# The start of a two-block forward pass on one core: loads by two queues, products of zeros, a fixed order of the first splits, the bias on GpSimd's queue

## The chip, the cores and the metric

One core of one Trainium2 chip. The metric is device microseconds of one execution, lower is better. The kernel before takes 864.13 us (median of three runs, 862.28 to 865.0).

## The reference, cut to what matters

A first block (neighbourhood attention and a bidirectional gated recurrence, then an MLP) and two further layers follow each other on 256 tokens of 1024 values, in float32. Only its start matters here:

```python
h = concatenate([meta_tokens, x])          # 16 meta tokens and 256 tokens, 1024 values each
a = rms_norm(h, norm_mix)                  # h * (mean(h*h) + eps)^-0.5 * norm_mix
(q_na, k_na, v_na, q_hg, z_f, z_b, i_hg, g_hg, gate_na, gate_hg) = split_cols(a @ w_in)
# neighbourhood attention: s = q k^T * scale + bias(rpb); the keys are a window of tokens and the meta tokens
# the branch hgrn2 ends with  o * gain * silu(g_hg)
```

`k_na` is needed for the meta tokens too (they are keys), `g_hg` is used for the 256 tokens alone.

## The kernel before, in words

**Products.** Float32 operands are split in two parts of type float32r, `hi` (a rounded copy, written by ScalarE) and `lo` (the rest, written by VectorE), and a product is three TensorE products: hi by hi, hi by lo, lo by hi. All weights come as one stream of half units (512 rows by 512 columns, 1 MB), in the order of use: `gh` (columns of g_hg), `kn` (k_na), `qn` (q_na), `vn` and so on, two half units each. `emit_raw` (L215) loads half units into three buffers `raw`, by SyncE's queue; `emit_hl` (L238) splits them by quarters into six buffers `whi`, `wlo` (L252 on ScalarE, L253 on VectorE). `use` (L325) hands a half unit to the products. `gh` is made by `xstat_unit`: x^T chunks are the stationary operand, 24 products of 128x512 for each of two halves of the tokens (L347 to L349). `kn` is made by `wstat_unit`: weights are stationary, x^T chunks with 272 columns (256 tokens and 16 meta tokens) stream, 96 products (L357 to L359).

**The start (L486 to L547).** SyncE's queue loads the first tokens `h[0]` in two halves, the row `grow` (norm_mix), the identity, the weights' first quarter, the second tokens `h[1]`, the second quarter, and so on. TensorE spreads `grow` over the partitions (L496). `norm_in` (L515): ScalarE squares and sums (L438), VectorE adds (L429), GpSimd takes the power -0.5 (L430), VectorE scales both halves of the columns (L525, into `xn`). `split_in` (L528): TensorE transposes four blocks (L406), `split_bank` writes `xh` on ScalarE (L413) and `xl` on VectorE (L414). `meta_in` (L549) does the same for the 16 meta tokens `hm`: L525 into `xnm`, transposes L553, then 16 columns of `xh` and `xl`. `ev_gh` (L562) evicts gh: a tanh on ScalarE (L564), two VectorE operations (L565, L566).

**Bias.** `bias_loads` (L602) loads eight pieces `braw` of the bias table (32 partitions, 8 rows of 133 values for each partition; 133 KB) by SyncE's queue (L608), and GpSimd adds the window mask (L613).

**Order.** Each engine runs its instructions strictly in the order of the program that was built. A scheduler with estimated costs sets that order when the program is built; `tc.issue_after` adds a rule that something comes behind a named instruction. A queue's loads start in the order of their issue.

Of the kernel before, what the change touches and what calls it, by code (L numbers as in the profile page):

```python
# [37 lines left out]
# rows of the vector array (128 values each)  # L38
# [3 lines left out]
def consts():  # L42
# [5 lines left out]
    for i in range(7):  # L48
        # the pairs of tokens that a block of 2^(i+1) tokens has across its middle
        a, b = p[:, None] >> i, p[None, :] >> i  # L50
        c[:, 128 * i:128 * i + 128] = (a ^ b) == 1
# [7 lines left out]
    # [s, t] within a tile: the pairs of a 64-chunk with s <= t, and the next chunk's whole  # L59
    c[:, C_GLA:C_GLA + 128] = p[:, None] <= t[None, :]  # L60
    # [s, t]: 1/16 where s <= t in one 64-chunk
# [7 lines left out]
def kernel(  # L69
# [25 lines left out]
    # Slots that tiles of disjoint lifetimes take in turn: "m0".."m18", and the larger "l0".."l2".  # L95
# [6 lines left out]
    def ta(p=128, n=512, dt=F32):  # L102
        """A short-lived tile of the main stream."""
        return tmp.tile([p, n], dt, name=nm("ta"), tag="ta", bufs=TA)

    def tb(p=128, n=512, dt=F32):
        """A short-lived tile of the work beside it."""
# [5 lines left out]
    def mps():  # L113
        return mp.tile([128, 512], F32, name=nm("mp"), tag="mp")
# [14 lines left out]
    # ------------------------------------------------ constants and vectors  # L129
# [17 lines left out]
    # the activation tables, before the first data  # L147
    S.activation(out=small([128, 1]), in_=zero1, func=AF.Square)

    # ------------------------------------------------ the stream of weights  # L150
    # A half unit is 4 chunks of 128 rows by 512 columns; it is split in two quarters.
# [62 lines left out]
    def emit_raw(n):  # L214
        while st["raw"] < min(n, len(units)):  # L215
# [4 lines left out]
            # the first ones by quarters, which are there sooner  # L220
# [5 lines left out]
    # Quarters that lie in free slots instead of the pool's buffers.  # L226
# [6 lines left out]
    def capped(key):  # L233
        """No splits from the unit key on are emitted."""
# [4 lines left out]
    def emit_hl(i0):  # L239
        """Splits quarters as far as the pool's buffers go, from quarter i0 on."""  # L240
# [17 lines left out]
    # Steps of an eviction that need TensorE again wait for the products of the next half unit.  # L258
# [20 lines left out]
    def flushed(n):  # L279
        """The deferred steps come here on TensorE, before the products of the body."""  # L280
# [8 lines left out]
    # Work beside the stream of products; that of lbg has the lowest priority.  # L289
# [23 lines left out]
    def group():  # L313
        """A group of the stream's products: behind the products beside it of LAG groups ago."""
# [13 lines left out]
    def use(key, budget=None):  # L328
        """The four row chunks (hi, lo) of the next half unit, with the work ahead emitted."""
# [21 lines left out]
    def wstat(ps, xs, ws, b, first, last):  # L351
        """ps[cols, tokens] += weight chunks (stationary, block b of 128 columns) by x^T chunks."""
# [49 lines left out]
    def transposes(src, n=4):  # L402
        """[128 tokens, n*128] -> one bank [128, n*128] of transposed blocks."""
# [6 lines left out]
    def split_bank(ps, hi, lo, scale=None):  # L410
        """hi and lo (f32r views) of a bank, or of a float32 tile, of the same shape."""
# [1225 lines left out]
```

## Time and profile before

| | |
|---|---|
| median of three runs (862.28 to 865.0) | 864.13 us |
| profiled execution, span from its first to its last instruction | 864.1 us |
| profiled execution, its own time: no figure apart from the span, nothing is listed around it | 864.1 us |
| TensorE products, busy | 841.6 us, 97% of the span |
| VectorE, busy | 583.3 us, 68% |
| ScalarE, busy | 463.2 us, 54% |
| GpSimd, busy | 57.4 us, 7% |
| mean granted TensorE clock | 0.995 |

How to read it: the start of the span is 0 in all views. A row of the view in order of time gives the start, the duration, the engine (PE TensorE, PEld its weight loads, DVE VectorE, ACT ScalarE, POOL GpSimd, SPq SyncE's queue), the line, the operation, output<-inputs, how many, and in brackets the idle time before it and what ended it. TensorE's products overlap: the distance from one start to the next is what one of them takes. Shares are means over stages, so a stage is read in its own window.

### The profile page before, as it was taken

Reading aid. Unit: us, or ns where it says so; the run is one execution under the profiler, and the core shown is the slowest. Engines: PE = TensorE matmul, PEld = TensorE weight load, DVE = VectorE, ACT = ScalarE, POOL = GpSimd, SP = SyncE. Lnnn points to the kernel's source line nnn. Section 1 sums busy time; section 2 is a strip of 40 time slices with the busy share of each in tenths; the row PEclk is TensorE's granted clock in tenths of the full one; section 3 lists DMA queues with packets and bytes.
Section 4 is the critical chain, followed back from the end, with each engine's and each line's share of the span. In section 5 each row is a group of like instructions: output and inputs, shape, how many; then the busy total and the mean of one; then the engine's idle time right before and its main releaser. Section 6 shows DMA issues by size and latency. Waiting matters only on the chain.

```text
span 864.1 us, 12274 instructions
## 1 busy us (share of the span) xinstructions
PE 841.6 (97%) x4757; PEld 726.7 (84%) x4757; DVE 583.3 (68%) x838; ACT 463.2 (54%) x743; POOL 57.4 (7%) x134
## 2 busy tenths in 40 slices
PE   6999999999999999999999999989999999999996
PEld 4899998887888888888888988868789999888885
DVE  6746637983858996787666777788756556656643
ACT  6546545655547545556666545444567544555532
POOL 1700001001000000000011000000000000010001
PEclk9999999999999999999999999999999999999999
DMA  8964415441457998777627556988445444535521
GB/s 272 282 216 129 138 49 196 149 144 50 157 209 266 382 372 293 256 283 241 214 87 238 188 179 217 313 270 266 148 171 174 168 148 146 183 110 178 188 98 49
DMA packets 88974, 168.84 MB, mean 195 GB/s; under 512 B 4770, under 2 KB 9250, under 8 KB 88916
## 3 DMA queue, kind: packets, MB, share of 16 engines
q1 hardware_dynamic: 88244, 167.51, 57.4%
q8 instruction: 37, 0.61, 0.3%
q10 hardware_dynamic: 288, 0.52, 0.2%
q14 instruction: 21, 0.17, 0.1%
q0 software_dynamic: 384, 0.03, 0.0%
HBM read 167.00 MB, written 1.05 MB: 194 GB/s over the span
## 4 chain that ended last, share of the span: by engine, by line
PE 86%; DMA 7%; DVE 3%; ACT 2%; issue 1%; SPq 0%; POOL 0%; POOLq 0%; DVEq 0%; ACTq 0%
PE acc L347 15%; PE acc L348 15%; PE acc L349 15%; PE acc L357 6%; PE acc L358 6%; PE acc L359 6%; DMA adw<-in_ada_w_dram 4%; PE mp L347 3%; PE mp L348 3%; PE mp L349 3%; PE mp L406 3%; DMA raw<-in_w_in_dram 2%; PE mp L829 1%; DVE wlo L253 1%; DMA lvf<-in_cst_dram 1%
## 5 line engine op out<-in xcount | busy, mean ns | idle before, releaser
L253 DVE TENSOR_TENSOR wlo<-raw,whi 128x1024 fp32r<-128x1024 f32 x244 | 295.3, 1226 | 142.7 <-ACT whi L252 140.8
L252 ACT ACTIVATE whi<-raw 128x1024 fp32r<-128x1024 f32 x244 | 253.6, 1056 | 188.6 <-PE acc L349 94.6
L461 DVE SCALAR_TENSOR_TENSOR tb<-adw,csil,tb 128x512 f32<-128x512 f32 x96 | 70.8, 747 | 11.4 <-DMA adw<-in_ada_w_dram 10.3
L359 PE MATMUL acc<-xh,wlo 128*128 128x272 f32 (+1 forms) x224 | 65.2, 293 | 1.2 <-DVE wlo L253 1.2
L357 PE MATMUL acc<-xh,whi 128*128 128x272 f32 (+1 forms) x224 | 65.0, 292 | 0.5 <-DVE kT L637 0.3
L358 PE MATMUL acc<-xl,whi 128*128 128x272 f32 (+1 forms) x224 | 64.9, 291 | 0.0
L359 PE MATMUL acc<-oh,wlo 128*128 128x256 f32 x192 | 55.0, 287 | 0.0
L358 PE MATMUL acc<-ol,whi 128*128 128x256 f32 x192 | 54.6, 284 | 0.0
L357 PE MATMUL acc<-oh,whi 128*128 128x256 f32 x192 | 54.4, 283 | 0.0
L348 PE MATMUL acc<-wlo,yT 128*128 128x512 f32 (+1 forms) x128 | 49.1, 384 | 3.4 <-DVE wlo L253 3.4
L348 PE MATMUL acc<-wlo,hh 128*128 128x512 f32 x128 | 50.6, 395 | 0.0
L349 PE MATMUL acc<-whi,hl 128*128 128x512 f32 x128 | 50.5, 395 | 0.0
L347 PE MATMUL acc<-whi,hh 128*128 128x512 f32 x128 | 50.3, 393 | 0.0
L347 PE MATMUL acc<-whi,yT 128*128 128x512 f32 (+1 forms) x128 | 49.1, 385 | 0.0
L349 PE MATMUL acc<-whi,yT 128*128 128x512 f32 (+1 forms) x128 | 48.8, 383 | 0.0
L359 PEld LDWEIGHTS acc<-xh,wlo 128*128 128x128 f32 x224 | 42.8, 192 | 2.1 <-DVE wlo L253 1.6
L348 PE MATMUL acc<-wlo,oh 128*128 128x512 f32 x112 | 44.5, 397 | 0.0
L347 PE MATMUL acc<-whi,oh 128*128 128x512 f32 x112 | 44.2, 394 | 0.0
L349 PE MATMUL acc<-whi,ol 128*128 128x512 f32 x112 | 44.1, 394 | 0.0
L357 PEld LDWEIGHTS acc<-xh,whi 128*128 128x128 f32 x224 | 42.8, 192 | 1.6 <-issue 0.6
L347 PE MATMUL mp<-whi,uh 128*128 128x512 f32 x112 | 43.9, 394 | 0.0
L348 PE MATMUL acc<-wlo,eh 128*128 128x512 f32 x112 | 43.9, 392 | 0.0
(406 smaller groups left out, 1950.6 us busy)
## 6 DMA issues: line engine op xcount, KB each, us to landing
raw<-in_odd_in_w_dram SPq DMA_DIRECT2D x28, 1024.0 KB, 5.0
adw<-in_ada_w_dram SPq DMA_DIRECT2D x48, 512.0 KB, 6.4
raw<-in_w_in_dram SPq DMA_DIRECT2D x21, 1024.0 KB, 5.2
raw<-in_even_in_w_dram SPq DMA_DIRECT2D x20, 1024.0 KB, 5.0
raw<-in_w_up_dram SPq DMA_DIRECT2D x16, 1024.0 KB, 6.6
raw<-in_w_down_dram SPq DMA_DIRECT2D x16, 1024.0 KB, 7.5
raw<-in_even_out_w_dram SPq DMA_DIRECT2D x8, 1024.0 KB, 5.8
raw<-in_odd_out_w_dram SPq DMA_DIRECT2D x8, 1024.0 KB, 5.0
```

Source lines behind the costliest of these rows:

```text
L252: S.activation(out=hi.rearrange("p k n -> p (k n)"), in_=r, func=AF.Copy)
L253: V.tensor_tensor(out=lo.rearrange("p k n -> p (k n)"), in0=r, in1=f(hi.rearrange("p k n -> p (k n)")), op=ALU.subtract)
L347: T.matmul(ps, lhsT=xh, rhs=wh, start=first and k == 0, stop=False)
L348: T.matmul(ps, lhsT=xh, rhs=wl, start=False, stop=False)
L349: last_mm[:] = [T.matmul(ps, lhsT=xl, rhs=wh, start=False, stop=last and k == n - 1)]
L357: T.matmul(ps, lhsT=wh[:, c], rhs=xh, start=first and k == 0, stop=False)
L358: T.matmul(ps, lhsT=wh[:, c], rhs=xl, start=False, stop=False)
L359: T.matmul(ps, lhsT=wl[:, c], rhs=xh, start=False, stop=last and k == n - 1)
L406: last_t[:] = [T.transpose(out=ps[:, 128 * b:128 * b + 128], in_=src[:, 128 * b:128 * b + 128], identity=ident)]
L461: V.scalar_tensor_tensor(out=a, in0=w[:, k], scalar=csil[:, kk:kk + 1], in1=a, op0=ALU.mult, op1=ALU.add)
L829: T.matmul(pss[i][:, 128 * hd:128 * hd + 128], lhsT=Kc[:, hd, 128 * i:128 * i + 128], rhs=bass.AP(tensor=q.tensor, offset=q.offset, ap=ap[ ...
```

## The change

- `h[0]` (two halves) and `h[1]` are loaded by ScalarE's queue; SyncE's queue begins with `grow`, the first quarter of weights, the identity and the second quarter. The activation table is loaded behind the three issues.
- TensorE runs ten products of zeros (128x256, bf16) before the products with `grow` and twelve behind them, each behind the one before.
- `norm_in` is cut in two, `sums_in` and `scale_in`. `in_turn` runs a step so that its instructions on all engines are issued behind the last ScalarE and VectorE instruction of the step before it. The first steps (sums, scalings, the first four quarters, the transposes with their splits) are written in one order with it, and `meta_in` is the last step of that order.
- The splits of later quarters, and those of a small gate weight `glw`, come behind the last step (`behind`, `started`).
- The eight loads of the bias go to GpSimd's queue, behind the cast of `lvl` (which waits for the load of `lvf`).

```diff
-    S.activation(out=small([128, 1]), in_=zero1, func=AF.Square)
...
-    nc.sync.dma_start(out=h[0][:, 0:512], in_=x[0:128, 0:512])
+    for c in (slice(0, 512), slice(512, 1024)):
+        nc.scalar.dma_start(out=h[0][:, c], in_=x[0:128, c])
+    nc.scalar.dma_start(out=h[1], in_=x[128:256])
     nc.sync.dma_start(out=grow, in_=vecs[R_MIX:R_MIX + 8].rearrange("(a r) c -> a (r c)", a=1))
-    nc.sync.dma_start(out=h[0][:, 512:1024], in_=x[0:128, 512:1024])
-    nc.sync.dma_start(out=ident, in_=cst[:, C_ID:C_ID + 128])
...
     nc.sync.dma_start(out=w0v[:, 0:2], in_=units[0][1][:, 0:2])
-    nc.sync.dma_start(out=h[1], in_=x[128:256])
+    nc.sync.dma_start(out=ident, in_=cst[:, C_ID:C_ID + 128])
     nc.sync.dma_start(out=w0v[:, 2:4], in_=units[0][1][:, 2:4])
...
+    def warm_up(n):
+        ps = mps()
+        for _ in range(n):
+            with after(first):
+                first[:] = [T.matmul(ps[:, 0:256], lhsT=warm[:, 0:128], rhs=warm, start=True, stop=True)]
+    warm_up(10)
...
+    warm_up(12)
...
-    norm_in(0, h[0], 2)
-    first_split(1)
-    split_in(0, 0)
-    first_split(2)
-    norm_in(1, h[1], 1)
-    split_in(1, 0)
-    first_split(3)
-    split_in(0, 1)
-    first_split(4)
-    split_in(1, 1)
+    turn = {}
+    def in_turn(step, *args):
+        traced = nc.cur_bb.bb.instructions
+        n = len(traced)
+        with ExitStack() as es:
+            for ins in turn.values():
+                es.enter_context(tc.issue_after(ins))
+            r = step(*args)
+        for k in nc.cur_bb.bb.instructions[n:]:
+            if k.engine in (S.engine, V.engine):
+                turn[k.engine] = k
+        return r
+    r0 = in_turn(sums_in, 0, h[0], 2)
+    in_turn(scale_in, 0, h[0], r0, 0)
+    in_turn(first_split, 1)
+    r1 = in_turn(sums_in, 1, h[1], 1)
+    in_turn(split_in, 0, 0)
+    in_turn(scale_in, 1, h[1], r1, 0)
+    in_turn(first_split, 2)
+    in_turn(split_in, 1, 0)
+    for t, r in ((0, r0), (1, r1)):
+        in_turn(scale_in, t, h[t], r, 1)
+        in_turn(first_split, 3 + t)
+        behind[:] = in_turn(split_in, t, 1)
+    started = list(behind)
...
     xstat_unit([("gh", 0), ("gh", 1)], xT, ev_gh)
-    meta_in()
+    in_turn(meta_in)
...
-                nc.sync.dma_start(out=raw[32 * r:32 * r + 32], in_=src)
+                with after([lvl_made]):
+                    nc.gpsimd.dma_start(out=raw[32 * r:32 * r + 32], in_=src)
...
-    split_bank(glw, glr[:, :, 0:16], glr[:, :, 16:32])
+    with after(started):
+        split_bank(glw, glr[:, :, 0:16], glr[:, :, 16:32])
```

What it does to the order of the instructions. **VectorE, where the meta tokens are scaled**, in the program before (`xnm` is the scaled meta tokens, `whi`/`wlo` quarters of weights, `xl` the lower parts of x^T, `raw_114` the first half unit of kn):

```order
L253 TENSOR_TENSOR wlo_169<-raw_108,whi_168 128x1024
L253 TENSOR_TENSOR wlo_180<-raw_108,whi_179 128x1024
L429 TENSOR_REDUCE sm_271<-sm_267 16x1
L414 TENSOR_TENSOR xl_9_118<-mp_161,xh_8_117 128x4x128
L525 SCALAR_TENSOR_TENSOR xnm_123<-hm_111,sm_272,mp_100 16x512
L525 SCALAR_TENSOR_TENSOR xnm_123<-hm_111,sm_272,mp_101 16x512
L253 TENSOR_TENSOR wlo_196<-raw_114,whi_195 128x1024
L414 TENSOR_TENSOR xl_11_120<-mp_172,xh_10_119 128x4x128
```

and in the changed one (line 250 is the line 253 of before, 426 is 429, 411 is 414, 540 is 525, 600 and 601 are 565 and 566; `raw_138` and `raw_253` are the two half units of kn, `raw_338` the first of qn, `acc_219` and `acc_220` the sums of gh):

```order
L250 TENSOR_TENSOR wlo_222<-raw_138,whi_221 128x1024
L250 TENSOR_TENSOR wlo_226<-raw_138,whi_225 128x1024
L250 TENSOR_TENSOR wlo_256<-raw_253,whi_255 128x1024
L250 TENSOR_TENSOR wlo_260<-raw_253,whi_259 128x1024
L426 TENSOR_REDUCE sm_297<-sm_293 16x1
L411 TENSOR_TENSOR glr<-glw,glr 128x8x16
L600 SCALAR_TENSOR_TENSOR gg_216<-gg_216,acc_219 128x512
L600 SCALAR_TENSOR_TENSOR gg_216<-gg_216,acc_220 128x512
L601 TENSOR_TENSOR gg_216<-gg_216,hgn_b 128x512
L250 TENSOR_TENSOR wlo_341<-raw_338,whi_340 128x1024
L601 TENSOR_TENSOR gg_216<-gg_216,hgn_b 128x512
L540 SCALAR_TENSOR_TENSOR xnm_149<-hm_135,sm_298,mp_118 16x512
```

The scaling of the meta tokens stood among the first splits, ahead of kn's; it now stands behind all four splits of kn, the eviction of gh and one split of qn.

**TensorE, where gh ends and kn begins**, in the changed program (lines 344 to 346 are 347 to 349 of before, 354 to 356 are 357 to 359, 588 is 553; `vrow` is a table of vectors):

```order
L346 MATMUL acc_220<-whi_205,xl_14_146 128x512
L588 MATMUL mp_303<-ident,xnm_149 128x16 x4
L610 MATMUL mp_320<-ident,vrow 128x128
L588 MATMUL mp_303<-ident,xnm_149 128x16 x4
L354 MATMUL acc_348<-xh_11_143,whi_221 128x272
L354 MATMUL acc_349<-xh_11_143,whi_221 128x272
L354 MATMUL acc_350<-xh_11_143,whi_221 128x272
L354 MATMUL acc_351<-xh_11_143,whi_221 128x272
L355 MATMUL acc_348<-xl_12_144,whi_221 128x272
```

Before, the transposes of the meta tokens stood within gh, with 22 of its 48 products still to come; now nothing of gh is left behind them, and kn's products, which read the meta tokens' columns, follow at once.

**GpSimd**, in the changed program (427 is the power, 430 before; 608 is the cast of `lvl`):

```order
L427 TENSOR_TENSOR sm_170<-sm_169,mhalf 128x1
L608 CAST lvl<-lvf_317 128x896
L644 DMA braw_484<-in_na_rpb_dram 32x8x133
L644 DMA braw_509<-in_na_rpb_dram 32x8x133 x2
L644 DMA braw_484<-in_na_rpb_dram 32x8x133 x2
L644 DMA braw_509<-in_na_rpb_dram 32x8x133
L644 DMA braw_484<-in_na_rpb_dram 32x8x133
L644 DMA braw_509<-in_na_rpb_dram 32x8x133
L427 TENSOR_TENSOR sm_298<-sm_297,mhalf 16x1
```

The eight issues now stand ahead of the meta tokens' power, which before had only the two powers of the tokens in front of it. From the first products of qn on, the order on every engine is that of before (one product of qn stands some places later).

## Rows read from the trace of the kernel before

**Rows 1.** The page's head and its first part: span; busy time, share of the span and number of instructions of each engine.

```profile
span 864.1 us, 12274 instructions
PE 841.6 (97%) x4757; PEld 726.7 (84%) x4757; DVE 583.3 (68%) x838; ACT 463.2 (54%) x743; POOL 57.4 (7%) x134
```

**Rows 2.** Who TensorE waited for, whole span, three of the list, longest first: us in total, times, longest.

```profile
PE acc L348 <- DVE wlo L253: 3.4, 1, 3.4
PE acc L347 <- ACT xh L413: 2.5, 1, 2.5
PE acc L359 <- DVE wlo L253: 1.2, 2, 0.8
```

**Rows 3.** Stretches of 1 us: length, busy time (instructions) of PE, PEld, DVE, ACT, POOL, then the granted clock, the DMA engines' busy share, GB/s.

```profile
6.00:7.00 1.00, 1.00 (x2) 0.00 (x0) 0.22 (x2) 0.01 (x1) 0.55 (x1) 1.00 0.65 215
9.00:10.00 1.00, 0.00 (x0) 0.00 (x0) 0.59 (x1) 0.68 (x2) 0.00 (x0) 1.00 1.04 401
```

**Rows 4.** In order of time, the chain to the first product of gh.

```profile
0.72 1.28 ACT L148 ACT_TABLE_LOAD   x1 [0.72 <-PEq L1626]
3.51 0.63 ACT L438 ACTIVATE junk<-h 128x512 bf16<-128x512 f32 x1 [1.29 <-DMA h<-in_x_dram]
7.74 1.12 PE L406 MATMUL mp<-ident,xn 128*128 128x128 f32 x4 [0.66 <-DVE xn L525]
9.69 1.06 ACT L438 ACTIVATE junk<-h 128x1024 bf16<-128x1024 f32 x1 [0.32 <-DMA h<-in_x_dram]
11.38 0.80 PE L347 MATMUL acc<-whi,xh 128*128 128x512 f32 x1 [2.52 <-ACT xh L413]
```

**Rows 5.** In order of time, TensorE: products with the row of the norm, then products of gh (two places).

```profile
3.33 3.75 PE L496 MATMUL mp<-grow,one_row 1*128 1x512 f32 x4 [3.33 <-DMA grow<-in_vecs_dram]
12.40 0.63 PE L349 MATMUL acc<-whi,xl 128*128 128x512 f32 x1
12.83 0.63 PE L347 MATMUL acc<-whi,xh 128*128 128x512 f32 x1
16.29 0.39 PE L347 MATMUL acc<-whi,xh 128*128 128x512 f32 x1
16.52 0.39 PE L348 MATMUL acc<-wlo,xh 128*128 128x512 f32 x1
```

**Rows 6.** Groups by line and shape, from 0 to 26 us: busy us, mean ns of one, idle us before.

```profile
L253 DVE TENSOR_TENSOR wlo<-raw,whi 128x1024 fp32r<-128x1024 f32 x6 | 7.1, 1214 | 1.1 <-ACT whi L252 1.1
L252 ACT ACTIVATE whi<-raw 128x1024 fp32r<-128x1024 f32 x6 | 6.3, 1051 | 2.9 <-DMA raw<-in_w_in_dram 2.9
L414 DVE TENSOR_TENSOR xl<-mp,xh 128x512 fp32r<-128x512 f32 x4 | 2.7, 676 | 0.3 <-ACT xh L413 0.3
L413 ACT ACTIVATE xh<-mp 128x512 fp32r<-128x512 f32 x4 | 2.3, 573 | 0.0
L525 DVE SCALAR_TENSOR_TENSOR xnm<-hm,sm,mp 16x512 f32<-16x512 f32 x2 | 1.4, 732 | 0.1
L566 DVE TENSOR_TENSOR gg<-gg,hgn_b 128x512 f32<-128x512 f32 x1 | 0.7, 693 | 0.0
```

**Rows 7.** In order of time, the meta tokens and the first product of kn.

```profile
17.48 1.39 DVE L525 SCALAR_TENSOR_TENSOR xnm<-hm,sm,mp 16x512 f32<-16x512 f32 x2
17.48 0.65 PE L406 MATMUL mp<-ident,xn 128*128 128x128 f32 x4
20.86 0.67 PE L553 MATMUL mp<-ident,xnm 16*128 16x16 f32 x8
24.40 0.41 PE L357 MATMUL acc<-xh,whi 128*128 128x272 f32 x2
```

**Rows 8.** In order of time, the loads and splits of kn's second half unit, kn's products from the 50th (35.10) to the 96th and last (40.89), and the first product of qn.

```profile
13.95 5.16 SPq L608 DMA_DIRECT2D braw<-in_na_rpb_dram  x7
20.88 0.39 SPq L222 DMA_DIRECT2D raw<-in_w_in_dram  x1
35.10 0.28 PE L359 MATMUL acc<-xh,wlo 128*128 128x272 f32 x1
40.89 0.29 PE L359 MATMUL acc<-xh,wlo 128*128 128x272 f32 x1
41.45 0.35 PE L357 MATMUL acc<-xh,whi 128*128 128x256 f32 x1 [0.27 <-DVE kT L637]
```

**Rows 9.** From issue to landing, us (smallest, median, largest): the half units issued from 22 to 30 us; the one issued at 38.4 us.

```profile
DMA to landing us min/median/max: 11.1/11.2/11.2
DMA to landing us min/median/max: 5.2/5.2/5.2
```

**Rows 10.** In order of time, TensorE behind its longest wait.

```profile
575.15 0.80 PE L348 MATMUL acc<-wlo,yT 128*128 128x512 f32 x1 [3.36 <-DVE wlo L253]
576.17 0.63 PE L348 MATMUL acc<-wlo,yT 128*128 128x512 f32 x1
576.59 0.63 PE L349 MATMUL acc<-whi,yT 128*128 128x512 f32 x1
578.30 0.53 PE L347 MATMUL acc<-whi,yT 128*128 128x512 f32 x1
```

**Rows 11.** A split on VectorE in order of time, while GpSimd adds the bias; and the loads that GpSimd issues (ns smallest/median/largest, first and last start).

```profile
35.46 1.52 DVE L253 TENSOR_TENSOR wlo<-raw,whi 128x1024 fp32r<-128x1024 f32 x1
L453 POOL DMA_DIRECT2D tb<-in_ada_b_dram x12: 487/487/736, 139.9 to 473.2; - x12
```

More of the change, by code (lines that the diff above doesn't have):

```diff
@@ L487 @@
     grow = mt(10, [1, D], name="grow")
-    nc.sync.dma_start(out=h[0][:, 0:512], in_=x[0:128, 0:512])
+    for c in (slice(0, 512), slice(512, 1024)):
+        nc.scalar.dma_start(out=h[0][:, c], in_=x[0:128, c])
+    nc.scalar.dma_start(out=h[1], in_=x[128:256])
     nc.sync.dma_start(out=grow, in_=vecs[R_MIX:R_MIX + 8].rearrange("(a r) c -> a (r c)", a=1))
-    nc.sync.dma_start(out=h[0][:, 512:1024], in_=x[0:128, 512:1024])
-    nc.sync.dma_start(out=ident, in_=cst[:, C_ID:C_ID + 128])
     one_row = cp.tile([1, 128], F32, name="one_row")
-    G.memset(one_row, 1.0)
-    g_ps = [mps() for _ in range(2)]
-    for k in range(2):
-        T.matmul(g_ps[k], lhsT=one_row, rhs=grow[:, 512 * k:512 * k + 512], start=True, stop=True)
+    V.memset(one_row, 1.0)
     w0 = rawp.tile([128, 2048], F32, name="raw0", tag="raw")
@@ L504 @@
     emit_raw(2)
+    warm = mt(12, [128, 256], BF16, name="warm")
+    V.memset(warm, 0.0)
+    first = []
+    def warm_up(n):
[4 more added lines that the diff above has]
+    warm_up(10)
+    g_ps = [mps() for _ in range(2)]
+    for k in range(2):
+        with after(first):
+            first[:] = [T.matmul(g_ps[k], lhsT=one_row, rhs=grow[:, 512 * k:512 * k + 512], start=True, stop=True)]
+    warm_up(12)
     hm = mt(4, [16, D], name="hm")
@@ L508 @@
     emit_raw(NRAW)
+    S.activation(out=small([128, 1]), in_=zero1, func=AF.Square)
     xT = [(mt(0, [128, 4, 272], F32R, "xh0"), mt(1, [128, 4, 272], F32R, "xl0")),
@@ L513, with sums_in @@
     xn = [mt(5, [128, D], name="xn0"), mt(6, [128, D], name="xn1"), mt(7, [16, D], name="xnm")]
-    def norm_in(t, src, parts):
-        p = src.shape[0]
-        q = small([p, 3])
+    def sums_in(t, src, parts):
+        q = small([src.shape[0], 3])
         G.memset(q, EPS)
@@ L521, in norm_in, with scale_in @@
             sq_mean(src[:, n * i:n * i + n], q[:, i:i + 1], D)
-        r = rpow(q[:, 0:parts + 1])
-        for i in range(2):
-            c = slice(512 * i, 512 * i + 512)
-            V.scalar_tensor_tensor(out=xn[t][:, c], in0=src[:, c], scalar=r, in1=g_ps[i][0:p],
-                                   op0=ALU.mult, op1=ALU.mult)
+        return rpow(q[:, 0:parts + 1])
+    def scale_in(t, src, r, i):
+        c = slice(512 * i, 512 * i + 512)
+        V.scalar_tensor_tensor(out=xn[t][:, c], in0=src[:, c], scalar=r, in1=g_ps[i][0:src.shape[0]],
+                               op0=ALU.mult, op1=ALU.mult)
     def split_in(t, g):
@@ L530, in split_in @@
         c = slice(128 * t, 128 * t + 128)
-        split_bank(ps, xT[g][0][:, :, c], xT[g][1][:, :, c])
+        return split_bank(ps, xT[g][0][:, :, c], xT[g][1][:, :, c])
     def first_split(n):
@@ L536, in first_split @@
         cap[0] = 1 << 30
-    norm_in(0, h[0], 2)
-    first_split(1)
-    split_in(0, 0)
-    first_split(2)
-    norm_in(1, h[1], 1)
-    split_in(1, 0)
-    first_split(3)
-    split_in(0, 1)
-    first_split(4)
-    split_in(1, 1)
+    turn = {}
[23 more added lines that the diff above has]
+    started = list(behind)
     def meta_in():
-        norm_in(2, hm, 1)
+        r = sums_in(2, hm, 1)
+        for i in range(2):
+            scale_in(2, hm, r, i)
         ps = mps()
@@ L572 @@
     nc.sync.dma_start(out=lvf, in_=cst[:, 0:896])
-    G.tensor_copy(out=lvl, in_=lvf)
+    lvl_made = G.tensor_copy(out=lvl, in_=lvf)
     pv = mps()
```

## The prediction

> **What bounds the kernel now.** I read the page's head first: TensorE is busy 97% of the span [rows 1], so only what delays its products counts. The list of its waits comes next: of the waits that it names, 2.5 us stand before the first product of gh and 1.2 us in kn [rows 2]; the largest, 3.4 us, ends at 575.15 [rows 10], in a place that the change does not touch. So I then read the start in order of time, and there three things are to be seen. First, the chain to the first product: the second tokens arrive at 9.7, ScalarE squares them, and only then makes the first tokens' `xh`, whose transposes were done at 8.9; gh begins at 11.38 [rows 4]. Second, TensorE's level: gh's products start 0.43 us apart at 12.4 and 0.23 us apart at 16.3, the 1.2 and the 2.4 GHz levels (the granted clock is listed as 1.00 in both places, so the distances decide) [rows 3, 5]. Third, the bias: its loads stand in SyncE's queue ahead of kn's second half unit, which is issued at 20.88 and not at 13.95 [rows 8]. Behind the first product of qn, at 41.45, the order of everything is unchanged, and TensorE has hardly a gap to give. My forecast is therefore the shift of that one moment.
>
> **The sum.** Its base is the profiled execution, span 864.1 us, which stands at the median of the three runs.
>
> *The loads.* Of the three issues on ScalarE's queue, some 0.4 us each, then the table load, 1.28 us, the end comes at about 3.4, where the first tokens arrived before (3.51) [rows 4]: no cost. What counts is when `h[1]` lands. It cannot be worked out from one row. From 6 to 7 us the engines of the loads were busy 65% at 215 GB/s, with loads waiting, and from 9 to 10 full at 401 [rows 3]. If two queues fill them from the first packet (about 1.6), the 1 MB of tokens and as much of the weights beside them take 5.2 us: 6.9. If they change nothing, it stays 9.7. I take the middle, 8.2. The Trainium skill ("DMA: Bandwidth & Descriptors", section "Issuing engines are not separate DMA queues") says that loads from several engines run on the same 16 DMA engines and that only the sequencer's issue time is saved; by it `h[1]` would stay at 9.7 and the sum below be 1.5 us higher, while the 65% above leave room for more.
>
> *The first product* follows the landing by 11.38 - 9.69 = 1.7 us [rows 4]: 9.9.
>
> *The products of zeros* run from about 1.4 on, beside loads that nothing else waits for, and with the 3.75 us of the norm's row [rows 5] they keep TensorE at work until 8 or 9.5. That does bring a gain: I count gh at 0.23 us. Before, seven products at 0.43 [rows 5] and eight transposes cost some 1.9 us more; if the level falls again before gh, this comes back, 0 to 1.9.
>
> *gh in the fixed order.* `xh` takes 0.57, `xl` 0.68, a split 1.05 on ScalarE and 1.21 on VectorE, a scaling 0.73 [rows 6], four transposes 0.65 to their last result [rows 7]. Seven products and a wait of 0.3 for `xl`: 11.8. VectorE does `xl`, the second tokens' scaling and a split from 9.9 on: 12.5. Seventeen products, 3.9: 16.5. Transposes of the first tokens' second half, 0.65, and `xh`, 0.57: 17.7. Seven products and a wait of 0.3: 19.6. Transposes of the last piece and their `xh`: 20.9. Seventeen more products, which wait until 20.4 for a split, end gh at 24.3, against 27.0 before. So far the change wins almost 3 us.
>
> *The meta tokens.* kn's products read their columns. Before, VectorE scaled them at 17.48 and TensorE transposed them at 20.86, in the midst of gh, so that kn could begin at 24.40 [rows 7]. Now VectorE has the following in its queue behind `xl` of the last piece: four splits of kn, each behind its ScalarE half (first 20.9 + 1.05 = 21.9), 4.85 us: 26.8; two small ones, 0.5; three operations of gh's eviction, 0.69 each: 29.3; the first split of qn, 1.21: 30.5; the last operation of the eviction: 31.2; and only then the two scalings, 1.46: 32.7 [rows 6]. Another split (1.21) and a copy (0.27) stand before the first `xl` of the meta columns, 0.2: 34.4. Transposes and `xh` lie within that. TensorE has its last product of gh at 24.3 and nothing of kn that may run: it stands for about 9 us, but for four products that need `xh` alone. The rest of kn, 92 products at (40.89 - 35.10) / 46 = 0.126 us [rows 8], takes 11.6: qn begins at 46.0 and not at 41.45. **+4.6 us.**
>
> *The bias* no longer delays kn's weights; the second half unit is issued at about 13 and is there by 20. But VectorE is late by then, so this gives nothing beyond the 1.2 us of waits [rows 2], which the walk above no longer holds. GpSimd's queue has the eight issues ahead of the meta tokens' power: the cast of `lvl` ends at about 18.2, and with the 0.49 to 0.74 us of the nearest issues [rows 11] the eight are done by 24.1; the power is needed at 31.2. Cover 7 us, cost nothing; with issues above 1.6 us it is gone (below).
>
> *The clock behind the pause.* After a wait of 3.36 us TensorE's products ran 0.42 us apart until 578.3, 3.1 us [rows 10]; at the start it took from 11.38 to a point ahead of 16.29 [rows 4, 5], about 4 us. At 0.43 for 0.23, such a stretch loses 1.4 to 1.9 us; a pause of 9 us is longer than either needs. I take **+1.7**, between 0 (the level holds) and 1.9.
>
> *VectorE beside GpSimd.* The bias's additions now fall on 28 us and later, where VectorE is the bound; a split beside them took 1.52 for 1.21 [rows 6, 11]. On the 5 to 6 us of VectorE behind 28 that is 0 to 1.4; I take **+0.4**, as not every operation there showed it.
>
> *qn's first half unit* is issued when a raw buffer comes free, at about 20.4, and lands 5.2 to 11.2 us later [rows 9]: 25.6 to 31.6. ScalarE needs it at 27.9. 0 to 3.7; the bias's loads share the engines for part of it: **+0.4**.
>
> Sum: 4.6 + 1.7 + 0.4 + 0.4 = 7.1. **864.1 + 7.1 = 871.2 us**, 0.8% slower. About 0.3%, 2.6 us, is what a measurement of this kernel can tell from no change. Lowest: `h[1]` at 6.9 (-1.3), level held (-1.7), the last two at zero (-0.8): 867.4. Highest: `h[1]` at 9.7 (+1.5), gh at the low level (+1.9), the late half unit (+3.3), the rest 1.2: 879, which wants all at once; three of the four give 877.
>
> **The rivals.**
>
> *GpSimd's issues become the bound.* Each of the eight loads has 256 pieces where the load in the row has few; if an issue takes 2.0 us, the eight end at 34.2, the power at 34.8, and the scaling starts 3.6 us later: 874.8. For it: the row's 0.49 to 0.74 is for loads of 2 KB. Against: it needs more than twice the row's largest. Chance 0.12.
>
> *The other side: the meta tokens are not late.* If VectorE reached their scaling before gh's end (by 23.5), TensorE would go on with a pause of about 1.3 us for the transposes and the two splits of their columns, and qn would begin at 24.3 + 1.3 + 12.1 = 37.7: -3.7, 860.4 us. For it: gh ends almost 3 us sooner, and kn's weights wait for nothing. Against: VectorE's queue has 9.3 us of work between the last `xl` and the scaling, and it does not pass anything; the point from which it decides is that these 9.3 us would have to begin before 14.2. Chance 0.06.
>
> *Nothing to measure.* All at its lowest, 867.4, and the wait of 3.36 us at 571.8, which hangs on a load's landing, does not come back: 864.0. For it: such a wait depends on when loads meet. Against: everything there is shifted together. Chance 0.10, a third of it still above 0.3%.
>
> **How the numbers follow.** The forecast has 0.72. Slower by over 0.3%: 0.72 + 0.12 + 0.03 = 0.87; within 0.3%: 0.07; faster: 0.06. The range 867.5 to 877 takes in the forecast's bounds and the first rival; outside lie faster and same, 0.13, and a little above 877.
>
> **What would show it.** In the profile after: the first product of gh at 8.7 to 11.4, gh's products 0.23 us apart from the first on, gh's end at 23 to 26. Then TensorE's longest wait of the start, 7 to 10 us, ended by VectorE's scaling of `xnm`; VectorE without a gap from about 22 to 33; the first products of kn 0.23 us apart (the low level for kn, twice 0.126 less a little), then 0.126; qn's first product at 46 to 51. Whether the eight issues on GpSimd end before its power for the meta tokens is wanted, and qn's half unit before 28, settles two terms each by a row. I am wrong if kn begins within 3 us of gh's end, or if qn's first product comes later and the end does not.

## The result, and the profile after

The changed kernel takes 873.06 us (median of four runs, 872.36 to 876.98), the kernel before 863.29 us (four runs, 862.28 to 865.0): ratio 1.0114, interval 1.0085 to 1.0143, so 7.3 to 12.3 us slower. The forecast was 871.2 in a range of 867.5 to 877. The profiled execution has a span of 870.4 us and a time of 872.36; wherever a run lists both, the time stands about 2 us above the span. For the profile of before no time was listed, and I had set its span, 864.1, equal to its time. By that difference it was an execution of about 866 us (an estimate), some 2.5 us above the median.

The page's first part, to be held against [rows 1]:

```profile
span 870.4 us, 12333 instructions
PE 846.6 (97%) x4779; PEld 729.6 (84%) x4779; DVE 583.5 (67%) x840; ACT 462.8 (53%) x743; POOL 58.4 (7%) x141
```

TensorE is busy 97% as before and 5 us longer: the shares tell nothing. Whom TensorE waited for (us in total, times, longest), against [rows 2]:

```profile
PE mp L588 <- DVE xnm L540: 8.2, 1, 8.2
PE acc L345 <- DVE wlo L250: 1.5, 1, 1.5
```

One wait of 8.2 us heads the list, for the scaled meta tokens, where before the entries shown were 3.4, 2.5 and 1.2 us; the second entry is the wait at 582 that is spoken of below. TensorE in order of time, against [rows 4, 5, 7, 8]:

```profile
7.27 2.74 PE L509 MATMUL mp<-warm 128*128 128x256 bf16 x12
9.81 1.00 PE L403 MATMUL mp<-ident,xn 128*128 128x128 f32 x4
11.49 0.50 PE L344 MATMUL acc<-whi,xh 128*128 128x512 f32 x1 [0.69 <-ACT xh L410]
12.56 0.40 PE L344 MATMUL acc<-whi,xh 128*128 128x512 f32 x1
12.79 0.39 PE L345 MATMUL acc<-wlo,xh 128*128 128x512 f32 x1
...
25.67 0.40 PE L346 MATMUL acc<-whi,xl 128*128 128x512 f32 x1
34.29 0.58 PE L588 MATMUL mp<-ident,xnm 16*128 16x16 f32 x4 [8.22 <-DVE xnm L540]
36.12 1.27 PE L354 MATMUL acc<-xh,whi 128*128 128x272 f32 x4 [0.31 <-ACT xh L410]
...
50.63 0.28 PE L354 MATMUL acc<-xh,whi 128*128 128x256 f32 x1
```

gh ends at 26.1, kn begins at 36.12, qn at 50.63 and not at 41.45: 9.2 us later. VectorE over the same stretch shows why:

```profile
22.60 0.69 DVE L411 TENSOR_TENSOR xl<-mp,xh 128x512 fp32r<-128x512 f32 x1 [0.80 <-ACT xh L410]
23.55 4.63 DVE L250 TENSOR_TENSOR wlo<-raw,whi 128x1024 fp32r<-128x1024 f32 x4 [0.26 <-ACT whi L249]
...
28.36 1.27 DVE L600 SCALAR_TENSOR_TENSOR gg<-gg,acc 128x512 f32<-128x512 f32 x2
29.56 0.67 DVE L601 TENSOR_TENSOR gg<-gg,hgn_b 128x512 f32<-128x512 f32 x1
31.36 1.23 DVE L250 TENSOR_TENSOR wlo<-raw,whi 128x1024 fp32r<-128x1024 f32 x1 [1.14 <-ACT whi L249]
32.51 0.99 DVE L601 TENSOR_TENSOR gg<-gg,hgn_b 128x512 f32<-128x512 f32 x1
33.42 1.39 DVE L540 SCALAR_TENSOR_TENSOR xnm<-hm,sm,mp 16x512 f32<-16x512 f32 x2
```

From the end of the last `xl` to the start of the scaling `xnm` pass 10.1 us. They hold other work, in the order that the program was built with, and two gaps, of 0.26 and 1.14 us. Stretches of the change (length, busy time and count of PE, PEld, DVE, ACT, POOL, granted clock, DMA share, GB/s): the pause, the first part of kn, the rest of kn.

```profile
26.00:34.00 8.00, 0.07 (x1) 0.00 (x0) 6.87 (x10) 4.55 (x8) 3.58 (x5) 0.82 1.04 294
36.00:41.00 5.00, 4.88 (x21) 4.88 (x22) 2.06 (x10) 0.62 (x4) 5.00 (x15) 0.50 0.71 222
41.50:50.50 9.00, 9.00 (x73) 9.00 (x72) 3.44 (x9) 3.51 (x7) 1.66 (x5) 1.00 0.22 55
```

The pause costs twice: TensorE stands, and then it runs kn's first products at half the clock (1.2 GHz). GpSimd, and then the two places where ScalarE waited for a load, the first tokens' second half and qn's half unit:

```profile
18.51 0.93 POOL L608 CAST lvl<-lvf 128x896 uint8<-128x896 f32 x1 [7.41 <-DMA lvf<-in_cst_dram]
19.39 4.86 POOL L644 DMA_DIRECT2D braw<-in_na_rpb_dram  x8
28.32 0.57 POOL L427 TENSOR_TENSOR sm<-sm,mhalf 16x1 f32<-16x1 f32 x1 [4.07 <-DVE sm L426]
30.98 12.18 POOL L649 TENSOR_TENSOR bias<-braw,cs 128x160 f32<-128x160 f32 x24 [2.10 <-DMA braw<-in_na_rpb_dram]
```

```profile
6.88 0.63 ACT L435 ACTIVATE junk<-h 128x512 bf16<-128x512 f32 x1 [2.36 <-DMA h<-in_x_dram]
...
30.28 2.00 ACT L249 ACTIVATE whi<-raw 128x1024 fp32r<-128x1024 f32 x2 [1.73 <-DMA raw<-in_w_in_dram]
```

The eight issues take 0.61 us each and end at 24.25, 4 us before the meta tokens' power could run: it waits for VectorE, not for the issues. VectorE's gap of 1.14 us comes from qn's half unit: ScalarE waited for its landing and began to split it at 30.28.

Behind qn's first product not all was given on. The profiles are 9.1 us apart where TensorE's wait at 572 begins (581 in the change), and 6.3 at the end: in the change the wait at 582 is 1.46 us and no half clock follows, where before it was 3.36 us with a slow stretch [rows 10]. The first experiment asks whether that belongs to the change.

### The profile page after: what moved, and what is told of

The parts are those of the page before. It is cut to its first block, busy times and chain, and to the rows that moved or that the text cites. A ratio compares the mean times of both kernels' runs of the same rounds, so it can differ in the third digit from the quotient of the medians.

```text
span 870.4 us, 12333 instructions
## 1 busy us (share of the span) xinstructions
PE 846.6 (97%) x4779; PEld 729.6 (84%) x4779; DVE 583.5 (67%) x840; ACT 462.8 (53%) x743; POOL 58.4 (7%) x141
## 4 chain that ended last, share of the span: by engine, by line
PE 84%; DVE 5%; DMA 5%; ACT 3%; issue 2%; POOL 0%; POOLq 0%; ACTq 0%; DVEq 0%
PE acc L344 14%; PE acc L346 13%; PE acc L345 13%; PE acc L354 7%; PE acc L355 7%; PE acc L356 7%; DMA adw<-in_ada_w_dram 3%; PE mp L344 3%; PE mp L346 3%; PE mp L345 3%; PE mp L403 3%; DVE tb L458 1%; DVE wlo L250 1%; PE mp L865 1%; DMA raw<-in_w_in_dram 1%
## 5 line engine op out<-in xcount | busy, mean ns | idle before, releaser
L344 PE MATMUL acc<-whi,yT 128*128 128x512 f32 (+1 forms) x128 | 48.5, 380 | 0.0
L355 PEld LDWEIGHTS acc<-xl,whi 128*128 128x128 f32 x224 | 43.9, 196 | 0.2 <-issue 0.2
```

The source lines that it names most:

```text
L344: T.matmul(ps, lhsT=xh, rhs=wh, start=first and k == 0, stop=False)
L355: T.matmul(ps, lhsT=wh[:, c], rhs=xl, start=False, stop=False)
```

## The experiments

Each ran against the kernel before on the same chip in five rounds. Single executions of one kernel spread by 5 us and more, so an interval is about 0.2% to either side (0.3% in runs 9 to 11, with six executions each).

**1. The kernel before, again.** No edit.

> The kernel before, unchanged. Open: the profiled executions differ by 6.3 us (870.4 against 864.1), the medians by 9.8. Theory A: TensorE's wait of 3.36 us at 571.8 and the 3.4 us at half the clock behind it stand in the profiled execution of before and not in most others (the profile of the change has 1.5 us and no half clock there); then most spans here lie at 860 to 862.5 with a mean clock of 0.997, and those that have it at 863 or more with 0.995. Theory B: every execution has it, clock 0.995 and spans of 863 to 865 throughout, and the 3.5 us have another cause. Ratio 1.000 by both.

863.84 us, ratio 1.0011 (0.9992 to 1.0029). The profile has a span of 860.6, a wait of 1.60 us at 572.87 and no half clock there. Over its 12 executions the mean clock lies anywhere between 0.993 and 0.998, so neither theory is met in its numbers: the slow stretches come and go from one execution to the next. The 3 us given back behind 572 in the profile of the change therefore need not be an effect of the change, and 9.2 us at qn stands beside 9.8 us of the medians.

**2. The meta tokens out of the order.** The change with one word taken back.

```diff
-    in_turn(meta_in)
+    meta_in()
```

> The change with one word taken back: the meta tokens are not a step of the fixed order. Theory M (the meta tokens' scaling stands too far back in VectorE's queue, that is the whole loss): it is done before 20, kn begins within 1.5 us of gh's end, no stretch at half the clock at 31, qn's first product at 39 to 41.5 and not at 50.6: 860 to 864 us, ratio to before 0.996 to 1.001. Rival Q (the queues, the zeros or the loads on GpSimd cost it): the pause goes, and still qn begins at 45 or later, over 867 us, ratio above 1.004.

865.65 us, ratio 1.0033 (1.0015 to 1.0050), 7.4 us less than the change's median (7.0 by the two ratios). TensorE now waits for `xnm` nowhere. Its transposes come at 23.85, kn follows gh at once (28.84), qn's first product is at 43.84, between the two forecasts. But within kn TensorE still waits twice for the meta columns:

```profile
30.85 0.39 PE L355 MATMUL acc<-xl,whi 128*128 128x272 f32 x1 [1.60 <-DVE xl L411]
38.19 0.39 PE L355 MATMUL acc<-xl,whi 128*128 128x272 f32 x1 [0.78 <-DVE xl L411]
```

Their small `xl`, at 30.59 and 37.93, stand behind splits of kn and of qn in VectorE's queue. So the position of the meta tokens is most of the loss. The 2.4 us at qn that are left are not all the rest of the change: the place of these two `xl` is part of them.

**3. The meta tokens early in the order.**

```diff
     in_turn(split_in, 1, 0)
+    r2 = in_turn(sums_in, 2, hm, 1)
...
         in_turn(first_split, 3 + t)
-        behind[:] = in_turn(split_in, t, 1)
+        if t == 0:
+            for i in range(2):
+                in_turn(scale_in, 2, hm, r2, i)
+        in_turn(split_in, t, 1)
...
+    behind[:] = in_turn(meta_in)
...
-    in_turn(meta_in)
```

> The change with the meta tokens as early steps of the fixed order: their sums behind the second quarter, their scaling behind the third, their transposes and splits last, and kn's splits behind them. Theory M: VectorE does the scaling in its idle 17.2 to 19.3 at no cost, gh ends at 26 to 27, kn follows within 0.7 us at the full clock, qn's first product at 38.5 to 40: 2 to 3 us less than before, 859.5 to 862 us, ratio 0.995 to 0.999. Rival Q: above 867. If VectorE's two scalings (1.46 us) cannot lie beside TensorE's work, gh ends 1.4 us later and the ratio is 0.999 to 1.000.

862.14 us, ratio 0.9984 (0.9966 to 1.0002). qn's first product at 41.05. The fixed order is no loss by itself. But gh's last product starts at 28.42, where its end was forecast at 26 to 27. The level came up only at 15.29, for 10.62 in the change, so gh's first seven products are 0.43 us apart. The square of the meta tokens stands ahead of the third quarter's split on ScalarE, which puts that split on VectorE at 18.24 and the scaling `xnm` at 20.13, ahead of an `xl` for which TensorE then waits:

```profile
22.17 0.50 PE L346 MATMUL acc<-whi,xl 128*128 128x512 f32 x1 [0.72 <-DVE xl L411]
```

The longest wait of this profile for `wlo`, 2.35 us, lies at 572, far behind the start.

**4. Two queues alone.** The kernel before with the tokens on ScalarE's queue; SyncE's queue then begins with `grow` and the first quarter, and the table load comes behind ScalarE's three issues, as in the change.

```diff
-    nc.sync.dma_start(out=h[0][:, 0:512], in_=x[0:128, 0:512])
+    for c in (slice(0, 512), slice(512, 1024)):
+        nc.scalar.dma_start(out=h[0][:, c], in_=x[0:128, c])
+    nc.scalar.dma_start(out=h[1], in_=x[128:256])
...
```

> The kernel before with the tokens on ScalarE's queue and nothing else of the change. Theory L (two queues move the first MB sooner, but the weights then share the engines with the first tokens): the first tokens' second half at 6.9 and not at 5.3, the second tokens before 8 and not at 9.7; without the fixed order ScalarE has a split of weights ahead of the square of that second half, so the first product comes at 11.5 to 12.5 against 11.38: ratio 0.999 to 1.002. Rival R (what the Trainium skill states in 'DMA: Bandwidth & Descriptors': engines that issue are not separate queues of transfer): the second tokens stay at 9.7, ratio 1.000 to 1.001. Rival G (more bytes early are a gain): first product at 10, ratio 0.998.

863.61 us, ratio 0.9997 (0.9977 to 1.0018); first product at 11.80. The first 5.5 us of loads, first before, then here:

```profile
1.50:7.00 5.50, 3.67 (x4) 1.16 (x4) 0.22 (x2) 2.15 (x6) 1.41 (x17) 1.00 0.68 213
```

```profile
1.50:7.00 5.50, 3.75 (x4) 1.16 (x4) 0.00 (x0) 3.06 (x5) 0.86 (x16) 1.00 0.92 301
```

ScalarE's squares of the first tokens' second half and of the second tokens:

```profile
7.11 0.61 ACT L437 ACTIVATE junk<-h 128x512 bf16<-128x512 f32 x1
...
8.22 1.06 ACT L437 ACTIVATE junk<-h 128x1024 bf16<-128x1024 f32 x1 [0.41 <-DMA h<-in_x_dram]
```

Two queues fill the 16 engines 92% instead of 68%, and the second tokens are there by 8.2, not 9.7. The Trainium skill ("DMA: Bandwidth & Descriptors", section "Issuing engines are not separate DMA queues") says that issuing from several engines saves only the sequencer's issue time. The trace does not agree: from 5 to 7 us, with loads waiting in both kernels, the DMA engines moved 364 GB/s here, and 187 to 273 in the six profiles with one queue. Rival R, by which the second tokens stay at 9.7, falls. The gain is lost on the way: the first tokens' second half is squared at 7.11 and not at 5.29, behind a split of weights that now came first.

**5. The zeros alone.** The kernel before with `warm_up(10)` and `warm_up(12)` around the products with `grow`, as in the change.

> The kernel before with the products of zeros and nothing else of the change. In the six profiles so far TensorE's level came up at 15.4, 14.6 and 16.4 without zeros ahead of gh (or with tokens and zeros apart), and at 10.6, 16.0 and 15.3 with them. Theory Z (the zeros do not decide when the level comes up; it falls by chance into gh's first products or ahead of them): the first product at 11.4 as before, since ScalarE makes xh late anyway, the level up between 14 and 17 in the profile, ratio 0.999 to 1.001. Rival K (the zeros keep TensorE at the 2.4 GHz level for gh): seven products and eight transposes 1.9 us shorter, ratio 0.998. If the twelve zeros hold up the transposes past 10.5, the first product comes later than 11.4 and the ratio is above 1.001.

863.80 us, ratio 1.0009 (0.9989 to 1.0028). The trace's record of the granted clock begins with the first rise of the level; the views of stretches list 1.00 before it, although products are 0.43 us apart there. All times of the level here and below are from that record. By it the level did come up early, at 10.68, and it fell again at 14.09. The scheduler, with the zeros in its order, put both first transposes ahead of gh's first product, which comes at 13.90 and not at 11.38.

```profile
7.27 2.74 PE L511 MATMUL mp<-warm 128*128 128x256 bf16 x12
9.81 1.03 PE L406 MATMUL mp<-ident,xn 128*128 128x128 f32 x4
12.80 0.63 PE L406 MATMUL mp<-ident,xn 128*128 128x128 f32 x4 [1.97 <-DVE xn L539]
13.90 0.65 PE L347 MATMUL acc<-whi,xh 128*128 128x512 f32 x1 [0.47 <-ACT xh L413]
...
19.20 0.63 PE L347 MATMUL acc<-whi,xh 128*128 128x512 f32 x1
19.62 0.63 PE L348 MATMUL acc<-wlo,xh 128*128 128x512 f32 x1
```

Products at 19.2 are still 0.42 us apart. The time is that of theory Z, but not by its way (14 to 17); rival K falls. As the zeros changed the order too, this run does not price them alone; runs 7 and 8, and 11, do.

**6. The bias alone on GpSimd's queue.** The kernel before with the loads issued by GpSimd, behind the cast of `lvl`.

```diff
-                nc.sync.dma_start(out=raw[32 * r:32 * r + 32], in_=src)
+                with after([lvl_made]):
+                    nc.gpsimd.dma_start(out=raw[32 * r:32 * r + 32], in_=src)
```

> The kernel before with the eight loads of the bias on GpSimd's queue and nothing else of the change; the meta tokens' power stands ahead of them. Theory B (the loads of the bias hold up kn's second half unit): that half unit is issued at 14 to 15 and not at 20.88, kn's waits of 1.2 us go, the eight issues take 0.6 each, ratio 0.997 to 0.999. Rival P (GpSimd's additions then fall beside VectorE's splits and slow them, as in the change from 31 on): the waits stay, by VectorE, ratio 0.999 to 1.001.

862.71 us, ratio 0.9987 (0.9966 to 1.0007): not to be told from no change. The half unit is issued at 14.82, kn's waits are gone, and qn's first product waits 2.07 us for VectorE's copies of `kT` instead. These stand behind two splits that began only at 38.35, because ScalarE had waited 8.0 us for their weights to land (37.25); beside GpSimd's additions the two took 2.73 us, where two took 2.36 at 25.14. So theory B's steps came, and the time was lost again, mostly to a late load and by 0.4 us to what rival P names.

**7 and 8. Without and with the zeros.** The meta tokens' transposes and splits now come ahead of gh's last twelve products and of kn's splits, one half of the first tokens is on each queue, the split of the first transposes stands ahead of the second tokens' square. Run 8 is the same with the zeros.

```diff
-    for c in (slice(0, 512), slice(512, 1024)):
-        nc.scalar.dma_start(out=h[0][:, c], in_=x[0:128, c])
+    nc.scalar.dma_start(out=h[0][:, 0:512], in_=x[0:128, 0:512])
+    nc.sync.dma_start(out=h[0][:, 512:1024], in_=x[0:128, 512:1024])
...
-    warm_up(10)
...
-    warm_up(12)
...
+    in_turn(split_in, 0, 0)
     r1 = in_turn(sums_in, 1, h[1], 1)
-    in_turn(split_in, 0, 0)
...
+    in_turn(split_in, 0, 1)
+    r2 = in_turn(sums_in, 2, hm, 1)
+    in_turn(scale_in, 1, h[1], r1, 1)
...
+    behind[:] = in_turn(meta_in)
...
-    in_turn(meta_in)
...
```

> The change without the zeros, with one half of the first tokens on each queue, the first transposes' split ahead of the second tokens' square, the meta tokens' sums behind the third quarter, their scaling, transposes and splits ahead of gh's last twelve products and of kn's splits, and their power ahead of the eight loads on GpSimd. Theory M: the first tokens' second half by 5, the first product at 9.3 to 10, the level up at 14 to 17, gh's end at 25 to 26.5, kn at once behind it, qn's first product at 38 to 39: 3 us less than before, ratio 0.995 to 0.998. Rival: the scaling of the meta tokens behind the last xl is late for the transposes (a wait of over 1 us in gh), ratio 0.998 to 1.000.

> As the run before, with the ten and the twelve products of zeros. Theory Z: the twelve end at 9.8 where the first tokens' scaling is ready by 8 or sooner, so the first product comes 0.5 to 1.5 us later than without them, and the level comes up at 10.6 or at 14 to 17; ratio of this run 0.000 to 0.002 above that of the run without zeros. Rival K: the level is up for all of gh, 1.5 to 1.9 us shorter, ratio 0.001 below the run without zeros or less.

Without: 861.85 us, ratio 0.9976 (0.9953 to 0.9998). With: 865.08 us, 1.0018 (0.9998 to 1.0039), 3.2 us more. TensorE without, then with:

```profile
7.87 1.11 PE L403 MATMUL mp<-ident,xn 128*128 128x128 f32 x4
9.67 0.79 PE L344 MATMUL acc<-whi,xh 128*128 128x512 f32 x1 [0.69 <-ACT xh L410]
```

```profile
7.72 2.74 PE L509 MATMUL mp<-warm 128*128 128x256 bf16 x12
10.26 1.06 PE L403 MATMUL mp<-ident,xn 128*128 128x128 f32 x4
12.00 0.79 PE L344 MATMUL acc<-whi,xh 128*128 128x512 f32 x1 [0.69 <-ACT xh L410]
```

The first half of the first tokens' columns was scaled by 7.5 in both; the twelve products of zeros hold TensorE's queue until 10.26 and put off the first product by 2.3 us, and the level came up at 13.99 without and 16.94 with them. qn's first product: 40.13 and 42.72. Here the zeros are a cost. In run 7 qn was later than the 38 to 39 forecast, with a wait for a split within gh:

```profile
22.84 0.51 PE L345 MATMUL acc<-wlo,xh 128*128 128x512 f32 x1 [0.98 <-DVE wlo L250]
```

This is the fourth quarter's split, which comes behind the square of the meta tokens on ScalarE and took 1.78 us on VectorE (at 21.01). The longer wait for `wlo` in that profile, 2.76 us, lies at 573 and has nothing to do with the start; the expectation of run 12 takes it for this one.

**9 and 10. The rule alone, and with the bias.** The kernel before with the meta tokens behind the last split (9), and with the edit of run 6 as well (10).

```diff
...
-    split_in(1, 1)
+    last_split = split_in(1, 1)
...
-    meta_in()
+    with after(last_split):
+        meta_in()
```

> The kernel before with one rule added: the meta tokens come behind the last split of the first tokens, as in the change. The scheduler then puts their scaling right behind the last xl, ahead of gh's eviction and of kn's last two splits, since their power has GpSimd free. Theory C (it takes both, this rule and the loads of the bias ahead of the power on GpSimd, to bring the scaling behind kn's splits): kn begins 1 to 3 us after gh's end, no half clock there or a short one, qn's first product at 42 to 46, ratio 1.000 to 1.005. Rival S (the rule alone is the loss): a pause of 6 us or more, ratio above 1.008.

> The run before with the eight loads of the bias on GpSimd's queue as well. The scheduler now puts the scaling of the meta tokens behind kn's second half unit, gh's eviction and two splits of qn. Theory C: TensorE pauses 5 us or more between gh and kn, ended by VectorE's scaling, and goes on at the half clock for 3 us or more; qn's first product at 47 to 52, ratio 1.006 to 1.012, although each of the two edits alone costs little. Rival S: as the run before. If neither has a pause of 5 us, the loss in the change needs the fixed order too.

Run 9: 869.67 us, ratio 1.0078 (1.0048 to 1.0108). Run 10: 871.01 us, 1.0086 (1.0052 to 1.0120). Theory C falls: the rule alone, 0.78%, gives most of the 1.14% that the change loses. The two pause in different ways. TensorE in run 9, then in run 10:

```profile
31.39 1.05 PE L357 MATMUL acc<-xh,whi 128*128 128x272 f32 x3 [4.38 <-ACT xh L413]
36.94 0.60 PE L357 MATMUL acc<-xh,whi 128*128 128x272 f32 x1 [4.50 <-DVE gg L565]
```

```profile
32.56 0.57 PE L553 MATMUL mp<-ident,xnm 16*128 16x16 f32 x4 [5.52 <-DVE xnm L525]
34.38 1.28 PE L357 MATMUL acc<-xh,whi 128*128 128x272 f32 x4 [0.31 <-ACT xh L413]
```

ScalarE and VectorE in run 9:

```profile
28.54 2.00 ACT L252 ACTIVATE whi<-raw 128x1024 fp32r<-128x1024 f32 x2 [4.63 <-DMA raw<-in_w_in_dram]
...
31.12 0.21 ACT L413 ACTIVATE xh<-mp 128x64 fp32r<-128x64 f32 x1
```

```profile
29.63 4.35 DVE L253 TENSOR_TENSOR wlo<-raw,whi 128x1024 fp32r<-128x1024 f32 x1 [4.28 <-ACT whi L252]
...
36.21 0.67 DVE L565 SCALAR_TENSOR_TENSOR gg<-gg,acc 128x512 f32<-128x512 f32 x1
36.80 0.21 DVE L414 TENSOR_TENSOR xl<-mp,xh 128x64 fp32r<-128x64 f32 x1
```

In run 9 the scaling is done by 24, but the two small splits of the meta columns stand in ScalarE's and VectorE's queues behind splits of kn's second half unit, which landed only at 28.5, since the bias still holds up SyncE's queue. The first wait is for the meta columns' `xh`. The second ends with `gg`: TensorE has four places for sums (`accp`), gh's last sum holds the one that kn's fourth product writes, and gh's eviction, which frees it at 36.21, stands on VectorE behind the same splits. The products behind that one need the meta columns' `xl`, which starts only at 36.80. So the rule costs most of what the change loses, but by other waits. The profiled execution of run 9, 873.25 us, is also the slowest of its six; its split of 4.35 us, for 1.2 to 1.7 in the change and in run 10, makes some 3 us of the second wait (an estimate). In run 10 that half unit is there sooner, and the scaling itself is behind it, as in the change. In both the clock falls to half during the pause, for 13.7 and 6.8 us.

**11. The change without the zeros.** Both calls of `warm_up` taken out.

> The change without the products of zeros, nothing else. The pause between gh and kn stays (8 us, VectorE's chain behind the last xl). Theory Z (the zeros hold up the first transposes and do not bring the level sooner): first product 0.5 to 1.5 us sooner than 11.49, level up at 13 to 16, end 0.5 to 2 us sooner than the change: ratio to before 1.008 to 1.011. Rival K (the zeros give the 2.4 GHz level to gh): gh 1.5 to 1.9 us longer, ratio 1.012 to 1.014.

872.98 us, ratio 1.0110 (1.0083 to 1.0137): the change's own time. The first product is at 10.35, 1.1 us sooner, the level up at 15.47, and gh's last product starts at 26.42, 0.75 us later than in the change. Of the 1.1 us, 0.8 is the landing of the first tokens' second half, squared at 6.10 here and at 6.88 in the change; the zeros hold the transposes for about 0.5 us. gh takes 16.5 us from its first product, 1.9 more than in the change, which is what the level gave there. Still, the medians are the same. The pause of 7.8 us for `xnm` is there with and without the zeros.

**12. The meta tokens in the gap.** Run 7 with square and scaling of the meta tokens between the third quarter's split and the transposes behind it.

```diff
     in_turn(first_split, 3)
+    r2 = in_turn(sums_in, 2, hm, 1)
+    for i in range(2):
+        in_turn(scale_in, 2, hm, r2, i)
     in_turn(split_in, 0, 1)
-    r2 = in_turn(sums_in, 2, hm, 1)
```

> The best run so far (no zeros, first tokens' halves on both queues) with the meta tokens' square and scaling moved from behind the third quarter's products into the gap that ScalarE and VectorE had there (VectorE idle 17.0 to 19.0, ScalarE 15.5 to 18.4), so that they hold up neither the fourth quarter's split nor the transposes. Expected: TensorE's wait of 2.8 us for that split falls to 1 or less, gh's end at 26 to 27, qn's first product at 38 to 39.5, 1 to 2 us less than that run: ratio to before 0.994 to 0.997. If something else in gh waits then, it is 0.997 to 0.999 as before.

860.33 us, ratio 0.9971 (0.9949 to 0.9992), faster than the kernel before by 0.1 to 0.5%. VectorE, and kn's stretch:

```profile
17.75 1.39 DVE L538 SCALAR_TENSOR_TENSOR xnm<-hm,sm,mp 16x512 f32<-16x512 f32 x2 [0.65 <-POOL sm L427]
19.62 0.69 DVE L411 TENSOR_TENSOR xl<-mp,xh 128x512 fp32r<-128x512 f32 x1 [0.47 <-ACT xh L410]
```

```profile
27.00:38.90 11.90, 11.90 (x97) 11.90 (x96) 11.17 (x21) 7.71 (x14) 9.35 (x15) 1.00 0.87 276
```

The scaling lies in a gap of VectorE, and TensorE waits for no split in gh. kn begins at 26.84 and runs without a gap at the full clock; qn's first product is at 38.93, 2.5 us before that of [rows 8].

## Why the prediction was right

**The cause was right, and the place.** The forecast said that the meta tokens' scaling, behind kn's splits and gh's eviction on VectorE, would stop TensorE between gh and kn. The wait is there, 8.22 us, by `xnm`; taking the one step out of the order gives about 7 of the 9.8 us back (run 2), and adding the rule to the kernel before costs 0.5 to 1.1% (run 9), there by other waits. With rule and bias together the wait for `xnm` is there again (run 10).

**The sum at qn was 2 us short.** It had 46.0 for qn's first product, and with the three terms behind it 48.5; measured 50.63. By its steps:

- *The loads.* The second tokens were put at 8.2; runs 4 and 11 have them at 8.2 and 8.1. The step that failed is "the first product follows the landing by 1.7 us: 9.9". It followed the wrong landing. In the change the first tokens' second half is late, squared at 6.88 and not at 5.29, and the zeros hold the transposes until 9.81: first product 11.49, 1.6 us later than forecast and no sooner than before.
- *The zeros.* They were booked as a gain of 1.9 us, at risk. In the profile of the change the level was up from 10.62 and gh ran at 0.23 us a product. But over five profiles with zeros it came up at 10.62, 10.68, 15.29, 16.01 and 16.94, over nine without between 13.99 and 17.0: no gain to count on, although it came in the change, and a cost where the transposes are ready sooner (runs 7 and 8).
- *gh's length*, 14.4 us from the first product, measured 14.6.
- *VectorE's queue*, 11.8 us from the end of the last `xh` to the end of the scaling, measured 12.2. The terms "qn's half unit late" and "VectorE beside GpSimd" had 0.8 for the excess. Both causes are in the rows, 1.14 us of gap and 0.99 for 0.67 us in an eviction step; the rest of the queue was shorter than forecast. So by the end of the meta columns' first `xl`, 36.3 for 35.2, the 1.6 us had become 1.1.
- *GpSimd's issues.* Forecast to end at 24.1, measured 24.25, with some luck: the cast ended 1.2 us later than forecast, and the issues took 0.61 us where the largest of the row, 0.74, was counted. The rival that they decide falls.
- *The clock behind the pause*, 1.7 us. kn takes 14.5 us from its first product to qn's, and 12.1 at the full clock in run 12: 2.4 us, more than the upper bound of 1.9. The bound came from slow stretches of 3.1 and 4 us; behind a pause of 8 us the level stayed down until 41.3, 5.2 us into kn. The forecast also let kn's four products that need `xh` alone run within the pause. Their `xh` came at 35.84, hardly ahead of `xl`, and they took 36.12 to 37.19. These two make the other 1.0 us.
- *Behind qn nothing changes.* The order is almost the same, and the profiles still drew 2.9 us together, by the wait at 572 and the slow stretch behind it, which differ between executions: 3.36 us with a slow stretch and 1.60 without in two profiles of the kernel before, 1.46 without in the change and 2.57 with one in run 11. The base, a span taken for a time, happened to lie only 0.8 us above the median of before, so that the shift, 2.7 us too small, and the base together leave 871.2 at 1.9 us under the 873.06 measured.

**The rivals.** The meta tokens were not early, as the order said. "Nothing to measure" named the wait at 571.8 as the thing that could hide the loss; in the profile it hid a third of it, in the medians nothing that can be seen.

What stays open: the 2.4 us that run 2 still has at qn over the kernel before were not parted. In kn it waits 2.4 us for the meta columns' `xl`, where the kernel before waited 1.4 us for splits and for `gg`; what zeros, loads and scalings in the chain add is not shown, though runs 7 and 8 show that the zeros alone can make 2.6.

## What to carry to other kernels

When an order is fixed by hand, ask of each step what is queued ahead of it on every engine it uses, and who reads its result first: a step with 1.4 us of work, left as the last of the order, cost about 7 us (run 2) because the next big products read the 16 columns that come of it. Put such a step where its engine has a gap that the trace shows. And hold a product of zeros against the first real instruction behind it in the same queue: filler that ends after the data is ready is a delay.

## What the runs showed of the hardware that was not expected

- *Two issuing engines moved more bytes*, 291 to 301 GB/s from 1.5 to 7 us in the change and in runs 2, 3, 4 and 11, for 213 to 236 in six profiles with one, and still the data that was wanted first came later: the first tokens' second half was squared between 6.04 and 7.78 us, for 4.69 to 5.31.
- *A VectorE split took 4.35 us* for 1.22 (run 9, at 29.63), while GpSimd's additions ran from 25.6 to 36.1. The Trainium skill ("Trainium Architecture — The Big Picture", section "What this means for kernel authors") says that VectorE and GpSimd share a pair of ports by an exclusive lock; the row is in keeping with that, but it does not show it: a split beside the same additions took 1.23 us in the change (31.36) and 1.52 before [rows 11], and no run here sets the cause of the 4.35 us apart.
- *A pause is paid for again at half the clock*: 3.4 us behind a wait of 3.4 us [rows 10], 5.2 us of kn behind the 8.2 us, and in run 9 a stretch that lasts to 43.1 behind two waits of 4.4 and 4.5 us. It does not follow every wait: in run 3 a wait of 2.35 us at 572 has no slow stretch behind it, in run 4 one of 1.84 us has.
